# A two-layer decoder trunk: the overflow block of its expert stage moved to the sixth pair, scatter blocks spread among weight chunks

## The chip, the cores and the metric

The kernel runs on one core of one Trainium2 chip. The metric is the time of one launch on the device, in microseconds. A core has five engines that run their own instruction queues and meet at semaphores: TensorE (PE, with its weight loads listed as PEld), VectorE (DVE), ScalarE (ACT), GpSimd (POOL) and SyncE (SP), which here issues nearly all loads. Working memory is SBUF, matmul sums land in PSUM, weights come from HBM by DMA.

## The reference, cut to what matters

256 tokens of width 2048 pass two layers. Layer 0 mixes by retention heads beside a causal convolution, layer 1 by sparse attention. Behind each mixer come a LayerNorm and a mixture of 16 experts, of which each token uses two, and a second LayerNorm:

```
for layer in range(2):
    m = mixer(h)                                   # even: retention + convolution; odd: sparse attention
    h = layer_norm(ALPHA * h + m)
    f = sum over e of gate[:, e] * ((silu(h @ gu_a[e]) * (h @ gu_b[e])) @ down[e])
    h = layer_norm(ALPHA * h + f)
```

All is fp32. The expert weights are 16 x (2048 x 1024 + 512 x 2048) x 4 bytes = 201 MB per layer.

## The kernel before, in words

All large tiles live in 22 pages of 1 MB. Weights come in chunks of one page; `pump` (L146) issues the next load on SP while fewer than `ringmax` chunks are held and a page is free, and `done_chunk` (L167) gives a page back. So SP's queue holds the loads in the order of use, each waiting for its page and for one of eight DMA semaphores.

The dense projections of the mixers split each fp32 weight into two reduced-precision parts (`split`, L222: a copy on ACT, a subtraction on DVE or POOL) and multiply three ways (`mm`, L242). `dense` (L272) runs the units in order.

An expert stage (`moe`, L821) first routes the tokens. Each expert takes up to 64 tokens; `back` (L836) copies the normalised input h into token rows of two pages. The 16 experts go in eight pairs (loop at L1016). For pair i:

- `gather` (L866) picks the tokens of both experts by matmuls with a one-hot matrix, h being the stationary side, in four blocks c; `gates` (L880) makes the matrices for the way back.
- `gu` (L897) is the first product of one expert: eight chunks, two columns of PE's array used side by side, into one PSUM bank; then SiLU on ACT and a product on DVE.
- `turn` (L914) transposes the result, ACT copies it to gT, and `down` (L934) multiplies by four chunks of the second weight. `weigh` (L924) scales by the gate into Y, hi part on ACT and lo part on DVE.
- `scatter` (L967) adds pair i's results to the rows of all tokens: eight blocks of four matmuls (`placed`, L950) and one DVE addition each (`spread`, L957). It runs in pair i + 1 behind the first `gu`, four blocks before the transpose and four after it.

Gathers of the next pair stand behind the first `down` and around the second transpose. Behind the last pair's second `gu` come `turn`, `overflow` and `last_down`. `overflow` (L1060) holds the general way for experts with more than 64 tokens, inside a conditional (L1070) on a count that is read into registers in pair 1; with these inputs it is branched past. Engines go through it one by one: PE, ACT and DVE branch and then set their semaphore to what the block would have left, and SP does so for each of the eight DMA semaphores, waiting first until the loads counted on it have landed. `overflow` takes three pages. `last_down` (L975) finishes the last expert column block by column block: `begin` puts the old sums of blocks 2 and 3 into PSUM by a matmul with the identity, four down products follow, each with `weigh`, and `finish` places the block and takes its LayerNorm statistics. In layer 0 two units of the next dense stage are split early within it.

In layer 1 of the trunk `fold` (L1115) normalises, transposes and scales two of sixteen column blocks at a time, `parts` (L1121) splits them, and the first dense matmuls start behind `parts(0)`. `norms` (L700) decides which quarter of the rows is normalised when.

Of the kernel before, what the change touches and what calls it, by code (L numbers as in the profile page):

```python
# [19 lines left out]
P = 128  # L20
# [9 lines left out]
TAPS = 31  # L30

# [49 lines left out]
class Trunk:  # L81
# [618 lines left out]
    def norms(self, kp):  # L700

        for c in ((0, 1), (2,), (3,))[kp] if kp < 3 else ():
            self.norm(c)
# [117 lines left out]
    def moe(self, layer, before_last=None):  # L821
# [14 lines left out]
        def back(t, c):  # L836
# [5 lines left out]
            o = h[t][:, c * 512:(c + 1) * 512]  # L842
# [23 lines left out]
        def gather(i, c):  # L866


            ps = self.psum("psg")
            for b in range(4):  # L870
                q, r = divmod(c * 4 + b, 2)
                for t in range(2):
                    f = h[t].rearrange("p (q j r) -> p q r j", q=8, r=2)[:, q, r, :]
                    nc.tensor.matmul(ps[:, b * P:(b + 1) * P], f, self.PT[i][:, t, 0:P], start=t == 0, stop=t == 1)
# [22 lines left out]
        def gu(i, j):  # L897
            ps = self.bank("pgu")
            for c in range(8):
                if i == 0 and j == 0 and c in (2, 4):  # L900
                    gather(0, c // 2 + 1)
# [55 lines left out]
        def spread(i, t, c):  # L957
# [3 lines left out]
            if i == 0:  # L961
                V.scalar_tensor_tensor(z, h[t][:, c * 512:(c + 1) * 512], ALPHA, ps, op0=ALU.mult, op1=ALU.add)
# [4 lines left out]
        def scatter(i, t):  # L967
            if i == 0 and t == 0:
                self.acc = [self.page(f"z{t}") for t in range(2)]
            for c in range(4):  # L970
                spread(i, t, c)
            if t == 1:
                self.drop(2)

        def last_down(gT, early):  # L975

            begun = {}

            def begin(b, alloc):

                for t in range(2):
                    ps = begun[b, t] = alloc("psb")
                    nc.tensor.matmul(ps, self.ident, self.acc[t][:, b * 512:(b + 1) * 512], start=True, stop=False, skip_group_check=True)  # L983
# [12 lines left out]
            begin(2, self.bank)  # L996
            ws = [self.take() for b in range(4)]
            for b in range(4):
# [8 lines left out]
                for half in range(2):  # L1007
                    weigh(7, 1, half, po, b * 256)
                for u in early if b == 2 else ():
                    self.split(u, nc.gpsimd)  # L1010
                    self.early.append(u)
                if b:
                    finish(b - 1)
                if b == 1:
                    begin(3, self.psum)
            finish(3)  # L1016
            self.drop(2)

# [4 lines left out]
        for i in range(8):  # L1023
            if i == 7:
                self.ringmax = 8
            if 0 < i < 7:
# [3 lines left out]
            sl = gu(i, 0)  # L1030
            if i:
                scatter(i - 1, 0)
# [369 lines left out]
```

## Time and profile before

| what | value |
|---|---|
| time, median of 3 runs | 1712.36 us (1707.39 to 1713.14) |
| the profiled execution | 1710.37 us, of it 1708.6 us span |
| mean granted TensorE clock | 0.983 of full |
| PE busy | 1639.9 us, 96% of the span |
| DVE, ACT, POOL busy | 743.3, 499.5, 345.4 us |
| moved by DMA | 528 MB, 309 GB/s over the span |
| first expert stage | from about 385 to 872 us |
| second expert stage | from about 1205 to 1692 us |
| split of a dense unit | ACT 1045 ns, POOL 2535 ns, DVE 1547 ns, means of the page |

Times within the span are counted from its start. In the rows below a line names its place in the code (L907 is line 907), its engine, the tile written and the tiles read, the partitions and elements, and how many instructions of the kind stand together. A time in brackets is idle time of the engine before the instruction, with the engine or transfer that ended it. TensorE matmuls overlap one another, so the distance of two starts says more than a duration.

### The profile page before, as it was taken

The numbers are of one execution on the slowest core, as the hardware profiler recorded it, in microseconds if no ns is written. First come the engines' busy times: TensorE is split into PE (matmuls) and PEld (weight loads), VectorE is DVE, ScalarE is ACT, GpSimd is POOL, SyncE is SP. The second block draws the span as 40 slices with busy tenths as digits, with TensorE's granted clock in tenths as the row PEclk, the third lists the DMA queues.
The fourth block names the chain that finished last, engine by engine and source line by source line (L and its number), as shares of the span: only waits on it lengthen the run. The fifth ranks groups of instructions, "written<-read, shape, count | busy, mean of one in ns | idle before, by whom it ended". The sixth has DMA issues, their size and how long they took to land. (4 is left out here: it accounts for less than half of the span.)

```text
span 1708.6 us, 21350 instructions
## 1 busy us (share of the span) xinstructions
PE 1639.9 (96%) x8551; PEld 1039.2 (61%) x8551; DVE 743.3 (44%) x1348; ACT 499.5 (29%) x780; POOL 345.4 (20%) x218
## 2 busy tenths in 40 slices
PE   9999999999999999999789999999999999999984
PEld 7888887786454445444268788788644445454432
DVE  5699987533123222221264675664412212232225
ACT  5434345433111111111054535553311111111101
POOL 1446664540000000000024554444000000000010
PEclk9999999999999999999989999999999999999996
DMA  9655545858999999999954554357899999999992
GB/s 341 216 196 173 172 148 192 304 197 353 376 411 421 421 421 420 422 420 420 407 186 139 171 176 145 124 200 267 319 358 416 422 420 421 421 421 420 421 413 76
DMA packets 122860, 528.29 MB, mean 309 GB/s; under 512 B 10506, under 2 KB 10898, under 8 KB 74498
## 3 DMA queue, kind: packets, MB, share of 16 engines
q1 hardware_dynamic: 122130, 525.32, 79.1%
q8 instruction: 71, 1.16, 0.3%
q0 software_dynamic: 480, 1.46, 0.2%
q14 instruction: 35, 0.29, 0.0%
q10 hardware_dynamic: 144, 0.07, 0.0%
HBM read 524.71 MB, written 2.10 MB: 308 GB/s over the span
## 5 line engine op out<-in xcount | busy, mean ns | idle before, releaser
L907 PE MATMUL pgu<-w,X 128*64 128x512 f32 x2048 | 449.8, 594 | 7.3 <-DMA w<-in_moe_w_gu_dram 7.3
L237 POOL TENSOR_TENSOR sp<-w,sp 128x1024 fp32r<-128x1024 f32 (+1 forms) x108 | 272.9, 2535 | 398.9 <-ACT sp L234 383.4
L907 PEld LDWEIGHTS pgu<-w,X 128*64 128x64 f32 x2048 | 144.0, 137 | 295.2 <-issue 267.3
L234 ACT ACTIVATE sp<-w 128x1024 fp32r<-128x1024 f32 (+1 forms) x228 | 230.4, 1045 | 121.4 <-PE acc L268 64.1
L237 DVE TENSOR_TENSOR sp<-w,sp 128x1024 fp32r<-128x1024 f32 (+1 forms) x120 | 185.3, 1547 | 129.4 <-ACT sp L234 129.1
L932 DVE SCALAR_TENSOR_TENSOR Yl<-pdn,gs,Yh 64x512 fp32r<-64x512 f32 (+1 forms) x136 | 97.7, 718 | 272.2 <-ACT Yh L931 271.2
L942 PE MATMUL pdn<-w,gT 128*64 128x512 f32 x960 | 212.6, 595 | 0.9 <-ACT gT L919 0.9
L931 ACT ACTIVATE Yh<-pdn,gs 64x512 fp32r<-64x512 f32 (+1 forms) x136 | 89.4, 657 | 306.9 <-PE pdn L942 213.0
L911 DVE TENSOR_TENSOR sl<-sl,pgu 128x256 f32<-128x256 f32 x32 | 13.5, 422 | 352.1 <-ACT sl L910 352.1
L266 PE MATMUL acc<-sp,xhi 128*128 128x512 f32 x384 | 152.2, 396 | 0.0
L267 PE MATMUL acc<-sp,xhi 128*128 128x512 f32 x384 | 149.7, 390 | 0.3 <-DVE sp L237 0.3
L268 PE MATMUL acc<-sp,xlo 128*128 128x512 f32 x384 | 149.8, 390 | 0.0
L792 POOL COPY pt<-pt 128x128 f32<-128x128 f32 x16 | 5.1, 317 | 707.1 <-DVE pt L791 707.1
L942 PEld LDWEIGHTS pdn<-w,gT 128*64 128x64 f32 x960 | 66.3, 137 | 123.4 <-issue 117.1
L910 ACT ACTIVATE sl<-pgu 128x256 f32<-128x256 f32 x32 | 12.3, 385 | 385.2 <-PE pgu L907 385.2
L470 DVE SCALAR_TENSOR_TENSOR pcv<-up,cw,pcv 128x255 f32<-128x255 f32 (+14 forms) x240 | 113.2, 472 | 7.3
L266 PE MATMUL acc<-sp,hhi 128*128 128x512 f32 x256 | 106.0, 414 | 1.2 <-ACT hhi L1125 1.2
L268 PE MATMUL acc<-sp,hlo 128*128 128x512 f32 x256 | 101.0, 395 | 1.2 <-DVE hlo L1126 1.2
L267 PE MATMUL acc<-sp,hhi 128*128 128x512 f32 x256 | 100.5, 393 | 0.0
L267 PEld LDWEIGHTS acc<-sp,xhi 128*128 128x128 f32 x384 | 72.2, 188 | 15.4 <-DVE sp L237 1.0
L268 PEld LDWEIGHTS acc<-sp,xlo 128*128 128x128 f32 x384 | 72.1, 188 | 15.3
L266 PEld LDWEIGHTS acc<-sp,xhi 128*128 128x128 f32 x384 | 72.2, 188 | 14.8 <-ACT sp L234 0.4
(305 smaller groups left out, 2067.8 us busy)
## 6 DMA issues: line engine op xcount, KB each, us to landing
w<-in_moe_w_gu_dram SPq DMA_DIRECT2D x256, 1024.0 KB, 16.5
w<-in_moe_w_down_dram SPq DMA_DIRECT2D x128, 1024.0 KB, 19.5
w<-in_even_w_in_dram SPq DMA_DIRECT2D x46, 1024.0 KB, 5.5
w<-in_odd_w_in_dram SPq DMA_DIRECT2D x32, 1024.0 KB, 5.2
w<-in_even_w_out_dram SPq DMA_DIRECT2D x16, 1024.0 KB, 8.7
w<-in_odd_w_out_dram SPq DMA_DIRECT2D x16, 1024.0 KB, 5.3
acc<-in_x_dram SPq DMA_DIRECT2D x8, 256.0 KB, 8.3
w<-in_even_w_in_dram SPq DMA_DIRECT2D x4, 512.0 KB, 6.7
```

The lines of the kernel that those rows point to most:

```text
L234: nc.scalar.activation(sp[:, 0], src, AF.Copy)
L237: eng.tensor_tensor(sp[:, 1], src, sp[:, 0].bitcast(F32), ALU.subtract)
L266: nc.tensor.matmul(ac, xh[:, x], wh, start=st, stop=False)
L267: nc.tensor.matmul(ac, xh[:, x], wl, start=False, stop=False)
L268: nc.tensor.matmul(ac, xl[:, x], wh, start=False, stop=en)
L470: nc.vector.scalar_tensor_tensor(y, up[:, c, 0:S - i], w, y, op0=ALU.mult, op1=ALU.add)
L907: nc.tensor.matmul(ps[h * 64:(h + 1) * 64, :], X[i][:, k, j * 64:(j + 1) * 64], wv[:, kk, :, h, :], start=k == 0, stop=k == KT - 1)
L910: nc.scalar.activation(sl, ps[:, 0:256], AF.Silu)
L911: V.tensor_tensor(sl, sl, ps[:, 256:512], ALU.mult)
L931: nc.scalar.activation(hi, po[r, :], AF.Copy, scale=g)
L932: V.scalar_tensor_tensor(lo, po[r, :], g, hi.bitcast(F32), op0=ALU.mult, op1=ALU.subtract)
L942: nc.tensor.matmul(po[b][half * 64:(half + 1) * 64, :], gT[:, c, h * 64:(h + 1) * 64], wv[:, half ^ j, 2 * b:2 * b + 2, :], start=kk == 0, ...
```

## The change

- `overflow` now stands behind the sixth pair (i = 5, `GENERAL`): that pair's second transpose and down product come first, then the block, then all gathers and the gates of the seventh pair. It uses two pages (one for weights instead of two); the two pages of h are given back at the top of the last pair. The ring is held at 14 chunks in the sixth pair and 16 after it.
- The eight blocks of a scatter are handed to the first `gu` of the next pair: one ahead of each of its chunks 2 to 7, one behind it before the transpose, one behind the transpose.
- `back` writes h in the order of the weights' rows, so a gather reads contiguous columns; the first scatter, which reads h, does so in two pieces of half the width through strided views.
- `begin` for blocks 2 and 3 runs ahead of chunks 3 and 5 of the last pair's second `gu`.
- The last `weigh` takes the upper half first; one unit instead of two is split early, and behind the four down products; ten warm-up matmuls follow `last_down`; the rows of the last LayerNorm are loaded before the last `gu`; `norms` takes one quarter per call.

```diff
@@ norms
-        for c in ((0, 1), (2,), (3,))[kp] if kp < 3 else ():
-            self.norm(c)
+        if kp < 4:
+            self.norm(kp)
@@ back
-            o = h[t][:, c * 512:(c + 1) * 512]
+            o = h[t][:, c * 512:(c + 1) * 512].rearrange("p (q r j) -> p q r j", q=2, r=2)
+            ps = ps.rearrange("p (q j r) -> p q r j", q=2, r=2)
@@ gather
-                q, r = divmod(c * 4 + b, 2)
-                for t in range(2):
-                    f = h[t].rearrange("p (q j r) -> p q r j", q=8, r=2)[:, q, r, :]
-                    nc.tensor.matmul(ps[:, b * P:(b + 1) * P], f, self.PT[i][:, t, 0:P], start=t == 0, stop=t == 1)
+                k = c * 4 + b
+                for t in range(2):
+                    nc.tensor.matmul(ps[:, b * P:(b + 1) * P], h[t][:, k * P:(k + 1) * P], self.PT[i][:, t, 0:P], start=t == 0, stop=t == 1)
@@ gu
-        def gu(i, j):
+        def gu(i, j, also=None):
             ps = self.bank("pgu")
             for c in range(8):
+                if also and c in also:
+                    also[c]()
...
@@ spread
             if i == 0:
-                V.scalar_tensor_tensor(z, h[t][:, c * 512:(c + 1) * 512], ALPHA, ps, op0=ALU.mult, op1=ALU.add)
+                for q in range(2):
+                    s = slice(q * 256, (q + 1) * 256)
+                    v = lambda x: x[:, s].rearrange("p (j r) -> p j r", r=2)
+                    V.scalar_tensor_tensor(v(z), h[t][:, c * 512:(c + 1) * 512][:, s].rearrange("p (r j) -> p j r", r=2), ALPHA, v(ps),
+                                           op0=ALU.mult, op1=ALU.add)
@@ scatter
-        def scatter(i, t):
-            if i == 0 and t == 0:
-                self.acc = [self.page(f"z{t}") for t in range(2)]
-            for c in range(4):
-                spread(i, t, c)
-            if t == 1:
-                self.drop(2)
+        def scatter(i):
+            def first():
+                if i == 0:
+                    self.acc = [self.page(f"z{t}") for t in range(2)]
+                spread(i, 0, 0)
+            def last():
+                spread(i, 1, 3)
+                self.drop(2)
+            return [first] + [lambda c=n // 2, t=n % 2: spread(i, t, c) for n in range(1, 7)] + [last]
@@ last_down
-            begin(2, self.bank)
...
-                for half in range(2):
+                for half in (1, 0):
                     weigh(7, 1, half, po, b * 256)
-                for u in early if b == 2 else ():
-                    self.split(u, nc.gpsimd)
-                    self.early.append(u)
                 if b:
                     finish(b - 1)
-                if b == 1:
-                    begin(3, self.psum)
+            for u in early:
+                self.split(u, nc.gpsimd)
+                self.early.append(u)
             finish(3)
             self.drop(2)
+            self.warm(10)
@@ the loop over pairs
+            if i == GENERAL:
+                self.ringmax = 14
             if i == 7:
                 self.ringmax = 8
+                self.drop(2)
...
-            sl = gu(i, 0)
             if i:
-                scatter(i - 1, 0)
+                sc = scatter(i - 1)
+                sl = gu(i, 0, {c: sc[c - 2] for c in range(2, 8)})
+                sc[6]()
                 gT = turn(sl)
-                scatter(i - 1, 1)
+                sc[7]()
...
             down(i, 0, gT)
-            if i < 7:
+            if i < 7 and i != GENERAL:
                 gather(i + 1, 0)
                 gather(i + 1, 1)
-            sl = gu(i, 1)
-            if i < 7:
+            if i == 7 and before_last:
+                before_last()
+            sl = gu(i, 1, {3: lambda: begin(2, self.bank), 5: lambda: begin(3, self.psum)} if i == 7 else None)
+            if i == GENERAL:
+                down(i, 1, turn(sl))
+                self.overflow(layer, rv, h, wide)
+                self.ringmax = 16
+                self.pump()
+                for c in range(4):
+                    gather(i + 1, c)
+                gates(i + 1)
+            elif i < 7:
...
-        gT = turn(sl)
-        self.overflow(layer, rv, h, wide)
-        if before_last:
-            before_last()
-        last_down(gT, self.units([Group(512, None, None)])[:2] if layer == 0 else ())
+        last_down(turn(sl), self.units([Group(512, None, None)])[:1] if layer == 0 else ())
@@ overflow
-        ow = [self.page(f"ow{i}") for i in range(2)]
+        ow = self.page("ow")
...
-        self.drop(5)
+        self.drop(2)
```

## Rows read from the trace of the kernel before

**Rows 1.** by stretch: busy us (instructions) of five engines, granted clock, DMA share, GB/s
```profile
465.00:826.00 361.00, 361.00 (x1968) 173.17 (x1966) 92.68 (x165) 56.90 (x99) 1.95 (x6) 1.00 1.01 420
...
850.00:856.00 6.00, 5.68 (x14) 2.41 (x16) 0.00 (x0) 0.00 (x0) 0.00 (x0) 0.50 1.05 386
...
858.00:866.00 8.00, 7.93 (x56) 4.72 (x52) 5.26 (x10) 3.05 (x6) 0.00 (x0) 1.00 0.54 177
...
879.50:883.40 3.90, 3.89 (x9) 3.08 (x10) 2.50 (x5) 2.93 (x5) 0.00 (x0) 0.50 0.00 0
```

**Rows 2.** PE in order of time, a pair of experts: start, us, what
```profile
632.07 13.90 PE L907 MATMUL pgu<-w,X 128*64 128x512 f32 x64
...
645.90 0.38 PE L954 MATMUL psa<-Yh,gtt 128*128 128x256 f32 x1
...
647.91 0.38 PE L917 MATMUL pst<-cst,sl 128*128 128x128 f32 x2
...
650.44 7.09 PE L942 MATMUL pdn<-w,gT 128*64 128x512 f32 x32
...
657.46 4.04 PE L874 MATMUL psg<-pt,acc 128*128 128x128 f32 x32
...
661.43 13.96 PE L907 MATMUL pgu<-w,X 128*64 128x512 f32 x64
...
679.40 0.60 PE L887 MATMUL psp<-cst,pt 128*128 128x128 f32 x4
...
687.64 0.60 PE L907 MATMUL pgu<-w,X 128*64 128x512 f32 x2
```

**Rows 3.** what PE waited for in each expert stage: us, times, longest
```profile
PE pgu L907 <- DMA w<-in_moe_w_gu_dram: 3.3, 6, 0.6
...
PE pgu L907 <- DMA w<-in_moe_w_gu_dram: 4.0, 8, 0.7
```

**Rows 4.** PE in order of time, end of the second expert stage
```profile
1660.75 1.94 PE L907 MATMUL pgu<-w,X 128*64 128x512 f32 x8 [0.65 <-DMA w<-in_moe_w_gu_dram]
...
1663.63 0.44 PE L917 MATMUL pst<-cst,sl 128*128 128x128 f32 x2 [0.94 <-DVEq L1070]
...
1679.43 1.88 PE L983 MATMUL psb<-z,cst 128*128 128x512 f32 x4
...
1681.24 1.95 PE L1005 MATMUL pdn<-w,gT 128*64 128x256 f32 x16
...
1683.12 0.39 PE L954 MATMUL psa<-Yh,gtt 128*128 128x256 f32 x1
...
1684.27 1.95 PE L1005 MATMUL pdn<-w,gT 128*64 128x256 f32 x16
```

**Rows 5.** ACT in order of time, the same place
```profile
1664.16 0.38 ACT L919 ACTIVATE gT<-pst 128x256 f32<-128x256 f32 x1 [1.04 <-PE pst L917]
```

**Rows 6.** PE, first product of the first pair, interrupted by gathers
```profile
407.60 3.65 PE L907 MATMUL pgu<-w,X 128*64 128x512 f32 x16
...
425.95 0.66 PE L887 MATMUL psp<-cst,pt 128*128 128x128 f32 x4
```

**Rows 7.** DVE in order of time, behind a down product
```profile
633.64 1.53 DVE L932 SCALAR_TENSOR_TENSOR Yl<-pdn,gs,Yh 64x512 fp32r<-64x512 f32 x2 [0.75 <-ACT Yh L931]
...
635.92 0.76 DVE L932 SCALAR_TENSOR_TENSOR Yl<-pdn,gs,Yh 64x512 fp32r<-64x512 f32 x1 [0.75 <-ACT Yh L931]
```

**Rows 8.** single lines: count, then ns least/median/most
```profile
L874 PEld LDWEIGHTS psg<-pt,acc x512: 193/197/197, 403.6 to 790.3; 128*128 128x128 f32 x171
...
L887 PE MATMUL psp<-cst,pt x64: 272/273/328, 425.9 to 1609.8; 128*128 128x128 f32 x64
...
L890 PEld LDWEIGHTS pgs<-gate,pt x128: 190/192/192, 426.3 to 1610.6; 128*128 128x128 f32 x128
...
L844 ACT ACTIVATE acc<-psh x6: 582/605/630, 400.7 to 403.1; 128x512 f32<-128x512 f32 x6
```

**Rows 9.** the branch past the conditional block, PE's sequencer: count, ns
```profile
L1070 PEldq COMPARE_BRANCH  x2: 6194/6326/6457, 843.7 to 1663.6; - x2
```

More of the change, by code (lines that the diff above doesn't have):

```diff
@@ L30 @@
 TAPS = 31
+GENERAL = 5
 C_ID, C_IOTA, C_TRI, C_SEL, C_KW, C_LOW, C_CAUS, C_N = 0, 128, 192, 320, 336, 352, 368, 496
@@ L965, in spread, with begin @@
             return z
-        def scatter(i, t):
-            if i == 0 and t == 0:
-                self.acc = [self.page(f"z{t}") for t in range(2)]
-            for c in range(4):
-                spread(i, t, c)
-            if t == 1:
-                self.drop(2)
-        def last_down(gT, early):
-            begun = {}
-            def begin(b, alloc):
-                for t in range(2):
-                    ps = begun[b, t] = alloc("psb")
-                    nc.tensor.matmul(ps, self.ident, self.acc[t][:, b * 512:(b + 1) * 512], start=True, stop=False, skip_group_check=True)
+        def scatter(i):
[5 more added lines that the diff above has]
+                spread(i, 1, 3)
+                self.drop(2)
+            return [first] + [lambda c=n // 2, t=n % 2: spread(i, t, c) for n in range(1, 7)] + [last]
+        begun = {}
+        def begin(b, alloc):
+            for t in range(2):
+                ps = begun[b, t] = alloc("psb")
+                nc.tensor.matmul(ps, self.ident, self.acc[t][:, b * 512:(b + 1) * 512], start=True, stop=False, skip_group_check=True)
+        def last_down(gT, early):
             def finish(b):
@@ L1023, in moe @@
         for i in range(8):
+            if i == GENERAL:
+                self.ringmax = 14
             if i == 7:
                 self.ringmax = 8
+                self.drop(2)
             if 0 < i < 7:
                 self.onehot(i + 1)
-            sl = gu(i, 0)
             if i:
-                scatter(i - 1, 0)
+                sc = scatter(i - 1)
+                sl = gu(i, 0, {c: sc[c - 2] for c in range(2, 8)})
+                sc[6]()
                 gT = turn(sl)
-                scatter(i - 1, 1)
+                sc[7]()
             else:
+                sl = gu(i, 0)
                 self.onehot(1)
@@ L1079, in overflow @@
                     for ab in range(2):
-                        w = ow[ab].rearrange("p (c n) -> p c n", c=KT)
+                        w = ow.rearrange("p (c r n) -> p c r n", c=8, r=2)
                         c0 = ab * FF + f * P
-                        nc.sync.dma_start(w, wg[ds(e, 1), :, c0:c0 + P].rearrange("o (c p) n -> p (o c) n", p=P))
+                        for r in range(2):
+                            nc.sync.dma_start(w[:, :, r, :], wg[ds(e, 1), :, c0:c0 + P].rearrange("o (c p r) n -> r p (o c) n", p=P, r=2)[r])
                         for k in range(KT):
-                            nc.tensor.matmul(ps[:, ab * S:(ab + 1) * S], w[:, k, :], at(k), start=k == 0, stop=k == KT - 1)
+                            nc.tensor.matmul(ps[:, ab * S:(ab + 1) * S], w[:, k // 2, k % 2, :], at(k), start=k == 0, stop=k == KT - 1)
                     nc.scalar.activation(gT[:, 4 + f, :], ps[:, 0:S], AF.Silu)
@@ L1088, in overflow @@
                 for c in range(4):
-                    w = ow[c % 2].rearrange("p (c n) -> p c n", c=4)
+                    w = ow.rearrange("p (c n) -> p c n", c=4)
                     nc.sync.dma_start(w, wd[ds(e, 1), :, c * 512:(c + 1) * 512].rearrange("o (c p) n -> p (o c) n", p=P))
```

## The prediction

> **What bounds the kernel now.** I read the page's slices first; both expert stages stand out there by their rate of loading. Whether that is the limit isn't said by a rate, so the next view is the table by stretch: for 361 us of the first expert stage PE is busy 361.00 us at the full clock while 420 GB/s flow [rows 1]. The PE rows of one pair of experts settle which of the two sets the pace. A pair takes 687.64 - 632.07 = 55.57 us [rows 2]. Its 24 loads of 1.049 MB need 24 x 1.049 / 0.420 = 59.9 us. So PE eats 4.3 us per pair out of the ring of prefetched chunks, and PE, not DMA, is the bound until the ring is empty. It is empty only at the very end: in the eighth pair PE waits for loads at eight chunks of the second layer (six in the first), at the 2.5 us spacing of the loads instead of 13.83 / 8 = 1.73 [rows 2, 3]. That is 6 x 0.77 = 4.6 us of stall in the first layer; in the second, by the idle time seen (4.0 against 3.3), 5.6. Then come the conditional block and the tail.
>
> So the reader is to see a PE-bound stage with some 5 us of slack per layer at its end, and a tail of 24.3 us behind the last down product (1684.27 to 1708.6 [rows 4]) that nothing here shortens.
>
> **The change, per layer.** All sums are against the profiled execution's own 1710.37 us (span 1708.6 and 1.8 around it); the median of the three runs shown is 2.0 above it.
>
> *Spread blocks among chunks (seven pairs).* Today eight blocks stand between the first product and its down product: 650.44 - 645.90 = 4.54 us, four blocks taking 2.01, so 0.50 each [rows 2]. They cover the latency of SiLU, product, transpose and copy. Uncovered, as at the end of the second layer, these cost: a group of eight started at 1660.75 would hand over at 1662.56 or so (1.81 later), the transpose came at 1663.63, so 1.07; the copy of gT ended 0.91 after it (1664.16 + 0.38), so with its hand-over 0.96 [rows 4, 5]. Two blocks of 0.5 fit inside these 2.03 us, so this stretch shrinks by 2.5. Six blocks move into the product: 6 x 0.50 = 3.0, plus a seam for each. The price of a seam stands in the one place where PE already leaves the product midway: 64 matmuls with two gather groups took 425.95 - 407.60 = 18.35 us, against 13.83 + 3.97 = 17.80 for the same work in two pieces [rows 2, 6]; 0.55 for two interruptions, of which a part is the slower first group. I take 0.22 each, 1.3 for six. Net 3.0 + 1.3 - 2.5 = +1.8 us per pair, **+12.6** for seven. Bounds: no seam 0.5 per pair (+3.5); the seam at 0.28 and a wait of 1.2 for Y in each pair 3.4 (+24). That wait: the first block is issued 2 x 1.71 = 3.4 us into the product; its half of Y is there at 634.4 (third DVE piece starts there), 2.3 us in, the whole of Y 4.6 us in (635.92 + 0.76 [rows 7]). I take the half, since the last pair's blocks already read one part of Y while ACT writes the next.
>
> The Trainium skill ("TensorE: Matmul & The Clock Gate", section Part 2) has TensorE pull the next weight load ahead of running matmuls when it goes to the background buffer. By that the seams cost nothing, the term is 3.5 instead of 12.6, and the sum below turns to -8 us; the 0.55 us of the interrupted product speak against it.
>
> *h in weight-row order.* A gather's weights are read contiguously instead of every second element. The nearest contiguous matmuls of the same size are four transposes that span 0.60 us, 0.27 of it the last one's own: one each 0.110. 32 gather matmuls span 4.04; with the same 0.27 for the last, one each 0.122 [rows 2, 8]: 64 x 0.012 = 0.8 us per pair. By the weight loads alone it is 197 against 192 ns [rows 8], 0.3 per pair. I take 0.6, nearer to the pace, eight times: **-5** (bounds 0 and -6.4). The price is paid in the copies of h out of PSUM, which now read every second element: six of 0.605 us on ACT per layer [rows 8]. No row shows a strided PSUM read; between 0 and a doubling (+3.6) I take 0, the contiguous row being the nearest. The first scatter's 16 half-size DVE operations in place of 8 lie beside 14 us of products; twice 0.68 us a block would still hide.
>
> The Trainium skill ("Advanced Engine Details and Errata", section Memory Cachelines) says that two hits on a 16-byte SBUF line keep full speed, and that PSUM wants two neighbouring fp32 values. By it a stride of two costs the gather nothing, so there is nothing to win, while the new PSUM read is the slow kind: the sum below is then +20 instead of +10. The 5 ns of the loads lean towards the page, the 0.122 against 0.110 away from it.
>
> *Overflow block behind pair 6.* PE's branch past the block took 6.2 and 6.5 us [rows 9]. Now it stands in the middle of a PE-bound stage: 6.3. There the gathers of the next pair no longer cover SiLU and gT: 2.03 - 0.22 for the transpose, 1.8. After the same pause in the tail the granted clock was 0.50 of full (1.2 GHz) from 850 to 856 us [rows 1]; PE's 5.7 us of work in it lose 2.8. Together **+10.9** (8.1 if the clock stays up, 13 if it stays down twice as long). SP also runs into the block: in the first layer it waits there until its eight loads have landed, and between 858 and 866 us the loads move 177 GB/s, (420 - 177) x 8 / 420 = 4.6 us lost [rows 1]. What is queued behind SP there are only later loads. PE has fourteen chunks allotted when it enters; its pause, gathers and gates take some 18 us, twelve chunks another 27, the SP drain (8 x 2.5 = 20) and the first new landing (5) are over 20 us before PE wants the fifteenth. So this stall costs nothing while PE is late.
>
> *Old sums into PSUM amid the last product.* Eight matmuls at the full clock, 1.81 for four [rows 4], plus two seams: **+3.8** in the product (bound 0, if PE still waits for loads there). They leave the tail.
>
> *Slack.* PE comes later to the last product, so the loads are there: **-4.6** and **-5.6**. With the terms above PE reaches the last chunk 12.6 - 5 + 10.9 + 3.8 = 22.3 us later than without stalls, 16.7 after today's time in layer 2; the load, delayed by 4.6, comes 12 us before that.
>
> *Tail from the transpose to the last down product.* Today 1684.27 - 1663.63 = 20.6 us in the second layer; I take the first as equal. Without branch and sums, at the full clock: 0.96, three down products of 1.88, two pairs of placed blocks of 1.15, and 0.3 of waiting for the first of them: 9.2 [rows 4]. **-11.4**.
>
> *Start of the odd layer.* One normalisation leaves the front (under 1 us), ten warm-up matmuls fill part of PE's gap before the transposes, and 3.9 us of dense matmuls ran at 0.50 of the clock [rows 1]; up to -4. Against it: only one unit is split early, so the second unit's split (1.05 us of ACT and 2.5 of POOL by the means of the page, queued behind the second block's parts) comes some 6 us after the first matmul, which at the full clock needs it after 3: +3. I take **-1** (from -4 to +3). The warm-up of the second layer and the earlier row loads lie beside DVE's last work.
>
> **Sum.** Layer 2: 12.6 - 5 + 10.9 + 3.8 - 5.6 - 11.4 = +5.3. Layer 1: the same with 4.6, less 1: +5.3. Together +10.6: 1721.0 on the profiled execution, 1723.0 on the median; I forecast 1721. In short, the block moves from one PE-critical place to another, and what is left is seams against gathers.
>
> **Rivals.**
> A, faster: *the seams vanish*, since weights for the next kind of matmul load behind the running one. Place: the six switches in each of 14 first products; price 18.2 us less: 1703. It decides once a seam costs under 0.1 us. For it: weight loads do overlap in steady runs. Against: the interrupted product. 20%.
> B, *no visible change*: gathers gain their 6, the clock stays up behind the block, seams at 0.18: 2 + 5.6 + 3.4 = 11 off the sum, 1712 on the median. 25%.
> C, slower than forecast: *the first spread block waits for all of Y*, PE in order behind it: 14 x 1.2 = 17 us, 1738; or the gathers gain nothing, 1731. For it: Y is one tile per half. Against: reads of parts in the last pair. 13% together.
> D, *the block starves PE*: were PE not late, SP's drain would show as a stall of up to 4.6 us per layer; it needs A to be true, and is inside it.
> My forecast has the remaining 42%.
>
> A measurement of this kernel can tell about 0.3%, 5.1 us. Faster than that: A, 0.20. Within: B, 0.25. Slower: the forecast and C, 0.55. The range runs from A at 1704 to C's 1737. The likeliest case's own range is 1716 to 1728.
>
> **What would show it.** PE still without waits up to the last product, and no wait for loads in it either. The pair period rising from 55.6 to about 56.8 us; first products of 18 us with six groups of four psa matmuls inside; gather groups of 32 under 3.97 us. PE's branch of about 6.3 us behind the sixth pair, a stretch at 0.50 of the clock after it, and a dip in GB/s some 25 us later. 9 to 10 us from the last transpose to the last down product. I am wrong if PE waits for loads in the eighth pair (then the stage is DMA-bound and the tail's gain stays), if the pair period doesn't rise, or if psa in the product waits for DVE.

## The result and the profile after

The changed kernel takes **1733.74 us** (median of four runs, 1731.84 to 1734.31) against 1710.57 before: ratio 1.0134, 95% interval 1.0113 to 1.0156. It is slower, as forecast, and inside the range; but the forecast was 1721, a loss of 10.6 us on the profiled execution where 23.4 came (span 1732.0 against 1708.6).

First the table by stretch of the changed kernel, columns as in [rows 1]: the second to seventh pair of the first layer with the first 7 us of the eighth, then the gathers behind the overflow block, and two stretches at the start of the odd stage.

```profile
466.00:826.00 360.00, 351.87 (x1856) 162.16 (x1852) 91.48 (x163) 54.25 (x93) 1.93 (x6) 0.99 1.00 413
...
748.80:755.50 6.70, 4.54 (x21) 4.57 (x22) 1.21 (x2) 1.28 (x2) 0.00 (x0) 0.50 1.02 415
...
890.30:895.20 4.90, 4.87 (x12) 3.77 (x13) 2.54 (x5) 3.94 (x6) 1.15 (x1) 0.50 0.00 0
902.40:905.50 3.10, 3.10 (x8) 2.48 (x8) 1.75 (x3) 1.35 (x4) 0.00 (x0) 0.50 0.21 52
```

PE is still the engine that sets the stage: busy 351.87 of 360 us, and most of the other 8 lie at the block. In 360 us it does 1856 matmuls, where 361 us held 1968 [rows 1]. In the waits of PE in the first expert stage and the turn behind it (us in all, times, longest) no wait for a load is left, nor is there one in the second stage; there were 3.3 and 4.0 us [rows 3]:

```profile
PE psg L875 <- DVEq L1090: 4.6, 1, 4.6
PE pst L920 <- DVE sl L914: 3.8, 9, 0.9
...
PE pdn L945 <- ACT gT L922: 1.0, 2, 0.5
```

So the loss is PE's own work and its order. One pair shows it. PE of the changed kernel in order of time, to be held against [rows 2]:

```profile
580.74 3.60 PE L910 MATMUL pgu<-w,X 128*64 128x512 f32 x16
584.27 0.38 PE L957 MATMUL psa<-Yh,gtt 128*128 128x256 f32 x1
...
592.54 1.94 PE L910 MATMUL pgu<-w,X 128*64 128x512 f32 x8
594.41 0.39 PE L957 MATMUL psa<-Yh,gtt 128*128 128x256 f32 x1
594.63 0.28 PE L957 MATMUL psa<-Yl,gtt 128*128 128x256 f32 x1
594.75 0.28 PE L957 MATMUL psa<-Yh,gtt 128*128 128x256 f32 x1
594.87 0.28 PE L957 MATMUL psa<-Yl,gtt 128*128 128x256 f32 x1
595.08 1.94 PE L910 MATMUL pgu<-w,X 128*64 128x512 f32 x8
...
600.49 0.44 PE L920 MATMUL pst<-cst,sl 128*128 128x128 f32 x2 [0.28 <-DVE sl L914]
...
601.46 7.09 PE L945 MATMUL pdn<-w,gT 128*64 128x512 f32 x32
608.48 3.84 PE L875 MATMUL psg<-pt,acc 128*128 128x128 f32 x32
612.25 13.95 PE L910 MATMUL pgu<-w,X 128*64 128x512 f32 x64
...
638.26 2.31 PE L910 MATMUL pgu<-w,X 128*64 128x512 f32 x10
```

The pair takes 638.26 - 580.74 = 57.52 us; it took 55.57. From the first product's start to the down product: 601.46 - 580.74 = 20.72 against 650.44 - 632.07 = 18.37 [rows 2], **2.35 us more**. The gathers behind the down product: 612.25 - 608.48 = 3.77 against 3.97; over the pair's three groups 0.39 less. 2.35 - 0.39 is the 1.95 by which the period grew.

A single place inside the product: a chunk of eight matmuls takes 594.41 - 592.54 = 1.87 us before it hands over to the block, where eight take 13.83 / 8 = 1.73 when the product runs through; the block takes 595.08 - 594.41 = 0.67, where blocks in a row take 0.50. So one interruption costs 0.14 + 0.17 = **0.31 us**, not 0.22. The starts tell where the second part sits: the block's first matmul is followed after 0.22 us and the others after 0.12, and the product resumes 0.21 after the last. The weight loads (PEld) of the same place:

```profile
594.41 0.19 PEld L957 LDWEIGHTS psa<-Yh,gtt 128*128 128x128 f32 x1 [0.81 <-issue]
594.52 0.19 PEld L957 LDWEIGHTS psa<-Yl,gtt 128*128 128x128 f32 x1
...
595.08 0.20 PEld L910 LDWEIGHTS pgu<-w,X 128*64 128x64 f32 x4
```

Inside the block a load starts 0.11 us ahead of its matmul (594.52 and 594.63). The block's first load starts with its matmul (594.41), and so does the product's first one behind the block (595.08): at a change of kind no load ran ahead.

Where the 23.4 us come from, in the two layers (forecast in brackets): spread blocks 7 x 2.35 = +16.45 each (12.6); gathers -3.1 each (-5); the sixth pair's excess over the fifth +8.4 and +9.1 (10.9); old sums +4.1 each (3.8); loads' waits -4.6 and -5.6 (the same); tail from the transpose to the last down product 9.3 us in both instead of 21.1 and 20.6, so -11.8 and -11.3 (-11.4); the start of the odd stage +3.8 (-1; measured below). That is 9.5 + 9.7 + 3.8 = 23.0. The rest is two short falls of the clock that come and go between runs, +1.15 ahead of the first expert stage and -0.95 in the odd stage.

### The profile page after: what moved, and what is told of

It reads as the page before. It is cut to its first block, busy times and chain, and to the rows that moved or that the text cites. A ratio compares the mean times of both kernels' runs of the same rounds, so it can differ in the third digit from the quotient of the medians.

```text
span 1732.0 us, 21420 instructions
## 1 busy us (share of the span) xinstructions
PE 1668.2 (96%) x8571; PEld 1037.4 (60%) x8571; DVE 756.9 (44%) x1364; ACT 499.1 (29%) x780; POOL 347.2 (20%) x218
## 5 line engine op out<-in xcount | busy, mean ns | idle before, releaser
L910 PE MATMUL pgu<-w,X 128*64 128x512 f32 x2048 | 466.0, 597 | 0.0
L910 PEld LDWEIGHTS pgu<-w,X 128*64 128x64 f32 x2048 | 137.4, 136 | 247.2 <-issue 230.6
L239 DVE TENSOR_TENSOR sp<-w,sp 128x1024 fp32r<-128x1024 f32 (+1 forms) x120 | 189.9, 1586 | 130.5 <-ACT sp L236 130.1
L971 DVE TENSOR_TENSOR z<-psa,z 128x512 f32<-128x512 f32 x104 | 71.7, 690 | 112.3 <-PE psa L957 112.0
L957 PEld LDWEIGHTS psa<-Yh,gtt 128*128 128x128 f32 x240 | 45.0, 188 | 81.9 <-issue 80.3
L269 PEld LDWEIGHTS acc<-sp,xhi 128*128 128x128 f32 x384 | 72.3, 188 | 15.4 <-DVE sp L239 1.0
```

Of the source, the lines that this page charges most:

```text
L239: eng.tensor_tensor(sp[:, 1], src, sp[:, 0].bitcast(F32), ALU.subtract)
L269: nc.tensor.matmul(ac, xh[:, x], wl, start=False, stop=False)
L910: nc.tensor.matmul(ps[h * 64:(h + 1) * 64, :], X[i][:, k, j * 64:(j + 1) * 64], wv[:, kk, :, h, :], start=k == 0, stop=k == KT - 1)
L957: nc.tensor.matmul(ps[:, o * 256:(o + 1) * 256], GT[i][0][:, o, t * P:(t + 1) * P], Y[i][n][:, o, c * 256:(c + 1) * 256], start=n == 0 and ...
L971: V.tensor_tensor(z, ps, z, ALU.add)
```

## The experiments

Theory T: the expert stage is PE's own, so each piece of PE time in the pairs counts; the interruptions are the largest piece that the forecast got too small, and the start of the odd stage is the second. R1: the block behind the sixth pair, with the drained load queue in it, holds the loss. R2: the start of the odd stage holds it. Times are medians; ratios are to the kernel before, in the same runs, with 95% intervals.

**a_behind**: the spread blocks back behind the product, in the old order.

```diff
-            return [first] + [lambda c=n // 2, t=n % 2: ...] + [last]
+            return [first] + [lambda c=n % 4, t=n // 4: ...] + [last]
...
-                sl = gu(i, 0, {c: sc[c - 2] for c in range(2, 8)})
-                sc[6]()
+                sl = gu(i, 0)
+                for f in sc[:4]: f()
                 gT = turn(sl)
-                sc[7]()
+                for f in sc[4:]: f()
```

> The changed kernel with one part undone: the eight spread blocks of a pair stand again in two fours behind the first product, before and after the transposes, instead of six of them between its chunks. Theory T (the spread blocks cost more than forecast): in the changed kernel the stretch from the first matmul of a first product to its down product is 20.72 us against 18.37 before, 2.35 us in each of 14 pairs, 33 us in all. T expects that stretch back at 18.4 us, and 1701 us if the loads keep up; the loads' waits that the kernel before had (4.6 and 5.6 us in its two layers) may come back, so 1701 to 1711. Rival R1 (the block behind the sixth pair, with the drain of the load queue in it, is what costs the most): the spread gives back no more than the 10 us by which the forecast was exceeded there, 1724 or more. Rival R2 (the start of the odd stage holds it): the same, 1724 or more.

Measured: 1702.45 us, ratio 0.9957 (0.9943 to 0.9971): 31.3 us less than the changed kernel, and faster than the kernel before. PE of this kernel in one pair:

```profile
576.76 13.90 PE L910 MATMUL pgu<-w,X 128*64 128x512 f32 x64
...
595.16 5.37 PE L945 MATMUL pdn<-w,gT 128*64 128x512 f32 x24
```

18.40 us again, and the period is 55.19. PE waits for no load in it. T holds; R1 and R2 fall as the main cause.

**a_twos**: the same six blocks, three places.

```diff
-                sl = gu(i, 0, {c: sc[c - 2] for c in range(2, 8)})
+                sl = gu(i, 0, {c: (lambda c=c: (sc[c - 3](), sc[c - 2]())) for c in (3, 5, 7)})
```

> The changed kernel with its six interleaved spread blocks in twos, ahead of chunks 3, 5 and 7 of the first product, so that there are three places where the product is interrupted in a pair and not six; all the blocks are still there. Theory T: a place costs 0.32 us whatever stands in it (chunk and block took 2.535 us in the changed kernel against 1.71 and 0.50 us by themselves), so 3 x 0.32 x 14 = 13 us less, 1720 us. Rival: the cost belongs to the block itself (its four matmuls run slower between chunks, 0.67 against 0.50 us), and stays with six blocks: 1733 us.

Measured: 1721.07 us, ratio 1.0067 (1.0048 to 1.0086). The pair takes 56.51 us, 1.01 less for three places fewer: 0.34 each. PE of this kernel:

```profile
584.20 0.39 PE L957 MATMUL psa<-Yh,gtt 128*128 128x256 f32 x1
...
585.35 3.65 PE L910 MATMUL pgu<-w,X 128*64 128x512 f32 x16
588.93 0.39 PE L957 MATMUL psa<-Yh,gtt 128*128 128x256 f32 x1
```

Two blocks together take 585.35 - 584.20 = 1.15 us, where two single ones take 1.34; two chunks together take 588.93 - 585.35 = 3.58, where two single ones take 3.74. The price is the place's and not the block's. (The 0.31 above is a little low, since the 13.83 and 2.01 it is held against each contain a change too.)

**b_scatter**: the kernel before with the interleaved blocks alone (the same edit as undone in a_behind, the other way round).

> The kernel before with one part of the change alone: six of a pair's eight spread blocks between the chunks of the first product. Theory T: seven pairs of a layer take 2.35 us more each, 16.45 us, and the loads' waits of the eighth pair (4.6 and 5.6 us) go, because PE now comes later than they do: +11.9 and +10.9, 1733 us. Rival (the forecast's own size, 1.8 us a pair): 12.6 less the same waits, 1725 us. Rival A of the prediction (no cost of a seam): 1710 us or less.

Measured: 1729.33 us, ratio 1.0119 (1.0095 to 1.0143). The period goes from 55.57 to 57.91 us, 2.34 more, and the loads' waits go. The 18 us are between the two expectations. From the first product to the last down product the first layer grew by 11.2 us in the profile, near T's 11.9, but the second by 7.0 instead of 10.9. The block still stands in the tail here, and PE's branch past it took 6.38 us in the first layer and 3.37 in the second (PE's sequencer, then the stretches of the two branches):

```profile
L1078 PEldq COMPARE_BRANCH  x2: 3374/4876/6377, 855.8 to 1685.5; - x2
```

```profile
855.80:862.20 6.40, 0.44 (x2) 0.20 (x2) 0.00 (x0) 0.38 (x1) 0.00 (x0) 0.86 0.99 364
1685.50:1688.90 3.40, 0.40 (x2) 0.17 (x2) 0.00 (x0) 0.38 (x1) 2.18 (x1) 1.00 0.02 5
```

PE was so late there that the loads had ended: 5 GB/s beside this branch, 364 beside the other. That one short branch is most of the 4 us by which T's sum was too high; by period and waits T holds. Why it was short is not shown.

**b_worder**: the kernel before with h in weight-row order alone; the first scatter reads h in halves, as in the change.

```diff
-            o = h[t][:, c * 512:(c + 1) * 512]
+            o = h[t][:, c * 512:(c + 1) * 512].rearrange("p (q r j) -> p q r j", q=2, r=2)
+            ps = ps.rearrange("p (q j r) -> p q r j", q=2, r=2)
...
-                    f = h[t].rearrange("p (q j r) -> p q r j", q=8, r=2)[:, q, r, :]
+                    nc.tensor.matmul(..., h[t][:, k * P:(k + 1) * P], self.PT[i][:, t, 0:P], ...)
```

> The kernel before with one part of the change alone: h in the order of the weights' rows, so that a gather reads its weights contiguously, the copies out of PSUM reorder, and the first scatter writes through strided halves. Theory T: the pair period falls by 0.38 us (gather groups of 32, 16 and 8 matmuls 0.20, 0.10 and 0.09 us shorter), 2.7 us in seven pairs, and PE waits that much longer for the loads in the eighth pair, since the loads set the time of the last chunk: 1710 us, within 2 us. Rival (the stage is bound by PE to its end): 1705 us. Rival (the copies out of PSUM with a stride of two cost twice): 1714 us.

Measured: 1707.08 us beside 1711.38, ratio 0.9981 (0.9968 to 0.9994). The period falls to 55.19, by 0.38 as expected, and PE comes to the eighth pair 2.9 us earlier. PE's waits for loads in this kernel, first and second layer:

```profile
PE pgu L907 <- DMA w<-in_moe_w_gu_dram: 5.0, 10, 0.6
...
PE pgu L907 <- DMA w<-in_moe_w_gu_dram: 6.0, 11, 0.7
```

They were 3.3 and 4.0 [rows 3]: 1.7 and 2.0 us of the gain are handed over to the loads, not all of it. The result is 0.9 us below T's band and 2 us above the PE-bound rival: neither holds as it stood.

**a_noblock**: the changed kernel without the overflow block, its branch and general path; the pages that it takes stay free.

```diff
-                self.overflow(layer, rv, h, wide)
+                wide("ohT", S), wide("ohT", S)
```

> The changed kernel without the block for overflowing experts (its branch, and so its general path, is left out; its two buffers are still taken, so that the rotation of buffers is the same, and the sixth pair keeps its order without overlap). Theory T: the pause of the branch (4.8 us from the end of the down product to the gathers beyond what other pairs show) and the half clock in the gathers behind it (2.0 and 2.7 us) go, the uncovered 1.7 us of the sixth pair stays: 7 us in each layer, 1720 us. Rival R1 (the block with the drained load queue starves later pairs too): more than the stretch itself, 1712 us or less. Rival: the pause only takes the place of waits for loads that would come anyway: 1730 us or more.

Measured: 1717.22 us, ratio 1.0049 (1.0032 to 1.0066). The sixth pair takes 59.03 instead of 65.92 us, and 59.04 instead of 66.65 in the second layer: 6.9 and 7.6 us, as T had it. What is left of its excess, 1.5, is the uncovered SiLU and gT. The other 2 us of the 16.5 are, by the two profiles, falls of the clock outside the experts.

**a_turned**: in the sixth pair the transposes ahead of the block, the down product behind it.

```diff
-                down(i, 1, turn(sl))
+                gT = turn(sl)
                 self.overflow(layer, rv, h, wide)
+                down(i, 1, gT)
```

> The changed kernel with the sixth pair's transposes and copy of gT ahead of the block, and its last down product behind it. In the changed kernel PE's gathers come 4.6 us after the down product, when DVE has done the last of four weighing steps. Theory T (the branch itself takes PE 6.3 us, and hides in the changed kernel under the running down product; only the weighing shows there): the down product starts 6.3 us after the transposes instead of 0.8, the gathers follow it at once instead of 4.6 us later: 0.5 to 1.5 us more in each layer, 1735 to 1737 us. Rival (the branch is short, and the pause is the weighing alone, which now stands beside PE's work): 3 to 4 us less in each layer, 1726 to 1728 us.

Measured: 1735.19 us, ratio 1.0142 (1.0112 to 1.0171). PE of the changed kernel at the block, then of this one:

```profile
738.26 0.44 PE L920 MATMUL pst<-cst,sl 128*128 128x128 f32 x2 [0.94 <-DVE sl L914]
739.23 7.09 PE L945 MATMUL pdn<-w,gT 128*64 128x512 f32 x32 [0.53 <-ACT gT L922]
750.96 9.58 PE L875 MATMUL psg<-pt,acc 128*128 128x128 f32 x64 [4.64 <-DVEq L1090]
```

```profile
738.50 0.44 PE L920 MATMUL pst<-cst,sl 128*128 128x128 f32 x2 [0.94 <-DVEq L1091]
744.84 9.05 PE L945 MATMUL pdn<-w,gT 128*64 128x512 f32 x32 [5.89 <-DMA w<-in_moe_w_gu_dram]
753.82 7.41 PE L875 MATMUL psg<-pt,acc 128*128 128x128 f32 x64
```

744.84 - 738.50 = 6.34 us from the transposes to the down product, and the sixth pair is 0.43 and 0.44 us longer in the two layers. (The profile puts the 5.89 down to a load, the one that came last.) The branch of PE's sequencer, in the changed kernel and in this one:

```profile
L1090 PEldq COMPARE_BRANCH  x2: 5947/6013/6079, 741.9 to 1573.2; - x2
```

```profile
L1091 PEldq COMPARE_BRANCH  x2: 5969/5993/6017, 738.5 to 1569.8; - x2
```

T holds. In the changed kernel the branch starts at 741.9, while PE still works on the down product, and is over some 6 us later; what shows is the time until DVE has done the last weighing step. DVE there, in the changed kernel:

```profile
747.72 1.53 DVE L935 SCALAR_TENSOR_TENSOR Yl<-pdn,gs,Yh 64x512 fp32r<-64x512 f32 x2 [0.75 <-ACT Yh L934]
750.00 0.76 DVE L935 SCALAR_TENSOR_TENSOR Yl<-pdn,gs,Yh 64x512 fp32r<-64x512 f32 x1 [0.75 <-ACTq L1090]
```

It ends at 750.76, PE's gathers start at 750.96.

**b_block**: the kernel before with the block behind the sixth pair, on one page fewer, with the gathers, ring sizes and pages given back as in the change; old sums in the tail.

```diff
+            if i == 5:
+                down(i, 1, turn(sl))
+                self.overflow(layer, rv, h, wide)
...
         gT = turn(sl)
-        self.overflow(layer, rv, h, wide)
```

> The kernel before with one part of the change alone: the block for overflowing experts behind the sixth pair instead of ahead of the last down product, with one load page fewer; the old sums still enter PSUM in the tail. Theory T: about 9 us more at the sixth pair, the tail from the transpose to the last down product 13 instead of 21 us, and the loads' waits of the eighth pair (4.6 and 5.6 us) gone: -4 in each layer, 1702 us. Rival R1 (the drain of the load queue behind the block brings waits for loads that are dearer than the forecast had it): 1712 us or more.

Measured: 1700.20 us, ratio 0.9945 (0.9924 to 0.9966). The sixth pair grows by 7.7 and 7.5 us, the tail falls to 11.9 us in both layers, and of the waits one of 0.6 is left in each:

```profile
PE pgu L907 <- DMA w<-in_moe_w_gu_dram: 0.6, 1, 0.6
```

R1 falls here for good: taken alone, the moved block is a gain of 5.6 us a layer.

**a_oddold**: the start of the odd stage as before.

```diff
-        if kp < 4:
-            self.norm(kp)
+        for c in ((0, 1), (2,), (3,))[kp] if kp < 3 else ():
+            self.norm(c)
...
-            for u in early:                     # behind the last down product, one unit
+                for u in early if b == 2 else ():   # amid it, two units
...
-            self.warm(10)
...
-        last_down(turn(sl), ...[:1] if layer == 0 else ())
+        last_down(turn(sl), ...[:2] if layer == 0 else ())
```

> The changed kernel with the turn from the first expert stage to the odd stage put back: two units split early on GpSimd amid the last down product instead of one behind it, the norms of columns in the old order, and no ten warming matmuls. Theory T: the milestones of the dense product lost 3.8 us between the end of the expert stage and its third unit, so 1730 us; not below 1727. Rival R2 (the odd start holds most of what the forecast lacked, about 10 us): 1724 us. Rival R3 (the old order is worse here, since the shorter tail leaves less time for two splits): 1735 us or more.

Measured: 1728.48 us, ratio 1.0117 (1.0091 to 1.0142). I take the stretch from the start of the last down product to the 114th matmul of the dense product, in its tenth unit: 47.31 us before, 51.12 in the changed kernel, 47.04 here. The 3.8 us are lost in this turn, and the old edits bring them back. Three single edits and one pair:

**a_early2** (two units behind the down product: `[:1]` to `[:2]`), **a_nowarm** (without `self.warm(10)`), **a_norms** (the old order of the norms alone), **a_amid** (two units amid the down product, new norms, warming kept).

> The changed kernel with two units split early behind the last down product instead of one. In the changed kernel the odd stage's start loses 3.8 us from the last down product to its fifth unit: PE stands for 2.2 us where DVE, sharing the time with GpSimd's late split of the second unit, is late with a norm, and runs 3.1 us at half clock behind that. Theory T (the one early unit is the cause): those 3.8 us go, 1730 us. Rival (the half clock at the first dense matmuls, there already, is the cause): no change in this loss, 1733 to 1734 us.

> The changed kernel without the ten warming matmuls behind the expert stage. They take 4.0 us (at half clock) of a gap of 9.5 us in which PE waits for the norms. Theory T: they neither delay the first transposes nor spare the half clock at the first dense matmuls, so nothing changes within 1 us: 1733 to 1734 us, and the start of the odd stage loses the same 3.8 us. Rival (they keep the clock from falling further): 2 us or more longer. Rival (they hold up the transposes): 1 to 3 us shorter.

> The changed kernel with the old order of the norms: two groups of columns before the first transposes, none before the fourth. Theory T: the norm that DVE was late with (2.6 us beside GpSimd) is then done before GpSimd's split starts; the 2.2 us gap goes and with it the half clock behind it, while the first transposes come up to 1 us later: 3 to 4 us less, 1730 us. Rival (only the split itself holds PE up): no change, 1733 to 1734 us.

> The changed kernel with its two early units split amid the last down product, as before; norms in the new order and the warming matmuls stay. From the last down product to the dense product's fifth unit the changed kernel loses 3.8 us, with two units behind the down product 5.1, with the old norms alone 2.3, with everything old -0.3. Theory T (the place of the early splits on GpSimd is what counts: amid the down product it is done with both before the columns' statistics come, and has no split left for the time in which DVE has norms): 0.5 to 1.5 lost, 1730 to 1731 us. Rival (the order of the norms is what counts): 2 to 4 lost, 1732 to 1734 us.

Measured: 1735.62, 1734.15, 1731.13 and 1731.22 us, two runs each. In that stretch they take, in one profile each, 52.45, 51.38, 49.60 and 47.95 us: +5.1, +4.1, +2.3 and +0.6 against the kernel before, where the changed kernel has +3.8. Of the four, a_early2 was a miss: with two splits ahead of them the columns' statistics come later on GpSimd, and the first transposes 2.3 us later. a_norms got 2.6 of the 3 to 4 us that its T expected. The ten warming matmuls do nothing for the time, as T had it: they run at half clock themselves, and in these two traces the dense product starts at half clock with or without them.

The others make a square (its corner with both old, a_oddold, also lacks the warming matmuls): new norms with the late split +3.8, old norms with the late split +2.3, new norms with two splits amid the down product +0.6, both old -0.3. So the place of the splits is worth 2.6 to 3.2 us and the order of the norms 0.9 to 1.5. The norms first: GpSimd, then DVE, of the changed kernel.

```profile
894.05 5.71 POOL L239 TENSOR_TENSOR sp<-w,sp 128x1024 fp32r<-128x1024 f32 x2 [8.28 <-ACT sp L236]
```

```profile
890.92 0.54 DVE L687 TENSOR_SCALAR z<-z,mv,rs 128x512 f32<-128x512 f32 x1
...
894.95 2.56 DVE L239 TENSOR_TENSOR sp<-w,sp 128x1024 fp32r<-128x1024 f32 x1 [1.20 <-ACT sp L236]
897.44 2.61 DVE L687 TENSOR_SCALAR z<-z,mv,rs 128x512 f32<-128x512 f32 x1
...
902.60 1.23 DVE L239 TENSOR_TENSOR sp<-w,sp 128x1024 fp32r<-128x1024 f32 x1 [0.25 <-ACT sp L236]
```

While GpSimd splits, DVE's own split takes 2.56 us instead of 1.23, and the last norm 2.61 where the one before took 0.54. PE stands for about 2 us until what DVE and ACT do behind that norm is done, and the clock is at half from 902.4 to 905.5 (the table at the top). With the old order this norm is done before GpSimd starts, and 0.9 us is left of the gap, where PE waits for the split itself; in a_amid, with the new order, it is there, behind the third unit's split.

The place of the splits acts by the split itself. With one unit split early, the lower part of the second unit's weights is the first of the two splits in the 894.05 row, and PE gets to it about when it is done. That the half clock at the first dense matmuls (890.3 to 895.2, the table at the top) hides this wait, a_noblock shows. Its code is the changed kernel's here, but its first dense matmuls run at full clock, and PE then waits for GpSimd:

```profile
882.60:886.90 4.30, 4.21 (x17) 2.78 (x17) 2.30 (x4) 3.33 (x6) 0.49 (x1) 1.00 0.01 2
```

```profile
886.38 0.50 PE L268 MATMUL acc<-sp,hhi 128*128 128x512 f32 x1
888.82 0.50 PE L269 MATMUL acc<-sp,hhi 128*128 128x512 f32 x1 [1.93 <-POOL sp L239]
```

The same matmul in the changed kernel:

```profile
896.49 0.50 PE L269 MATMUL acc<-sp,hhi 128*128 128x512 f32 x1
```

Counted from the start of the last down product (867.57 and 875.22) it comes after 21.25 and 21.27 us: the full clock gains nothing. In a_amid, with two splits amid the down product, it comes after 18.2.

Nor does the clock follow the place. It was at half there before [rows 1], and is so in b_block, both with two splits amid the down product; it is full in a_oddold, with the same place. b_block, then a_oddold, by stretch:

```profile
874.00:877.60 3.60, 2.99 (x7) 2.37 (x8) 1.86 (x4) 2.63 (x6) 0.00 (x0) 0.50 1.10 349
```

```profile
888.10:893.00 4.90, 4.90 (x22) 3.79 (x23) 3.49 (x6) 3.62 (x5) 0.24 (x1) 1.00 0.00 0
```

What sets the clock at this place these runs don't show.

**best1**: a_behind and a_oddold in one; what is left of the change is the moved block, the order of h, the old sums in the last product and two small edits (the upper half first in the last `weigh`, the earlier row loads). **best2**: b_block and b_worder in one, so without the old sums there and without the small edits.

> The changed kernel with two parts undone together: the spread blocks stand behind the first product in fours, and the turn to the odd stage is as before (two units split early amid the last down product, old order of norms, no warming matmuls). What is left of the change is h in weight-row order, the block behind the sixth pair and the old sums amid the last first product. Theory T (both causes are separate and add up): 1702.4 from the first alone less 4.3 from the odd start, 1698 us. Rival (the odd start lost because the spread made GpSimd and ACT late; with the blocks behind the product it costs nothing, so putting it back gives nothing): 1702 us.

> The kernel before with two parts of the change only: h in weight-row order, and the block behind the sixth pair. The spread blocks stand behind the first product, the old sums enter PSUM in the tail, the odd stage starts as before. Against the version with the old sums amid the last first product (1698.1 us) this prices that one part: it puts 4.1 us into the product (18.98 us with the sums against 14.9) and takes the tail from the transpose to the last down product from 11.9 to 9.3 us, since in the tail the first four of these matmuls cover the copy of gT. Theory T: a net loss of 1.5 us in each layer, so 1695 us without it. Rival (loads: with these sums gone PE reaches the last chunks sooner than they land, and waits): 1698 to 1700 us.

Measured: best1 **1698.11 us**, ratio 0.9931 (0.9910 to 0.9953); best2 1699.29 us, ratio 0.9925 (0.9911 to 0.9938). Both beat both kernels; which of the two is faster these runs don't tell, nor whether they are faster than b_block alone (1700.20): nearly all of the gain is the moved block. The two causes of best1 add up, as T had it. In best2 the rival was right: PE, earlier at the last product without the sums, waits for loads there, 1.7 and 1.9 us:

```profile
PE pgu L907 <- DMA w<-in_moe_w_gu_dram: 1.7, 3, 0.6
...
PE pgu L907 <- DMA w<-in_moe_w_gu_dram: 1.9, 4, 0.6
```

Where the old sums stand is then worth nothing that can be measured, the small edits included: 4.1 us in the product against 2.6 in the tail and the waits.

## Why the prediction was right in sign and wrong in size

**Spread blocks: the step that failed.** "I take 0.22 each." The mechanism and the other terms of this step hold: the blocks are read in PE's order, the first one doesn't wait for Y, and the uncovered stretch behind the product took 1.98 us (2.03 forecast). The term that failed is the size of the seam: 0.31 by the changed kernel's rows, 0.34 by a_twos, instead of 0.22. Six of them in 14 pairs make the term 2.35 us a pair instead of 1.8, 7.7 of the 12.8 us that the forecast lacks. The row that it came from [rows 6] gave 0.55 for two interruptions, 0.28 each; I argued a part of it away as the slow first group, with nothing that showed it. Rival A's place is settled too. The Trainium skill ("TensorE: Matmul & The Clock Gate", section Part 2) lets the next weights load ahead of running matmuls when they go to the background buffer, and the prediction took an interruption to be free by that. Here 42 places fewer gave 12.7 us back, 0.30 each, and at a change between these two kinds of matmul the first weight load starts with its matmul and not ahead of it; which buffer it goes to no row shows.

**h in weight-row order**: right in sign, -3.1 instead of -5 a layer. The pace of the four transposes was the wrong neighbour; the loads' own 197 to 192 ns [rows 8] were the nearer row (186 least and 192 median in the gathers after). The Trainium skill ("Advanced Engine Details and Errata", section Memory Cachelines) lets two hits on a 16-byte line of SBUF absorb the access latency, and wants every two consecutive elements in PSUM contiguous. By that, as the prediction read it, a stride of two fp32 values is free in the gathers' weights and slow in the copies (its +20 counts the gathers alone; copies at twice the time would add up to 3.6 us a layer). The runs show neither: the gathers gained 0.20 of 3.97 us, and the copies that now read PSUM with a stride cost the same 605 ns as in [rows 8]:

```profile
L847 ACT ACTIVATE acc<-psh 128x512 f32<-128x512 f32 x6 | 3.0, 605 | 0.0
```

**Overflow block**: 10.9 forecast, 8.4 and 9.1 measured. The branch isn't paid in full; it starts under the running down product, and DVE's weighing sets the 4.6 us that show (a_turned). The half clock behind it came as forecast, 6.7 us long. Rival D's stall did not come, not even in a_behind, where PE has no seams to be late with. The block came out 4.3 us cheaper in the two layers and the gathers gained 3.8 less: that these two misses nearly cancel is luck.

**Old sums, slack, tail**: 4.1 for 3.8, no wait left, 9.3 for 9.2. These held. The summary sentence behind the sum, that "the block moves from one PE-critical place to another", did not: with the loads' waits it was the part most worth having, 11 us in b_block (h in weight-row order alone gave 4).

**Start of the odd stage**: -1 forecast (bounds -4 to +3), +3.8 measured, 4.8 us of the miss. The late second split was seen, and its +3 is what the place of the splits measures (2.6 to 3.2). What failed is what it was set off against: the first dense matmul comes 15.1 us after the last down product, where it came after 14.7, the warming matmuls buy no time, and at full clock PE only waits longer for the split (a_noblock). One thing was not seen: DVE takes more than twice as long beside GpSimd, which makes a norm late that looked covered (0.9 to 1.5). Both edits are priced by the square above; what sets the clock there is open.

## What to carry to other kernels

In a stage where one engine is busy all the time, work put between its instructions isn't hidden by anything: price the change of kind itself, from a place where the kernel already does it, and multiply by the number of places before anything else. Where work must be interleaved, few places with much in each are cheaper than many. A price seen once for two places is to be taken whole, unless a row shows what else is in it. And before a stretch at half clock is counted as a loss, look at what the engine would wait for at full clock.

## What the runs showed of the hardware

- A change from the first product's matmuls (128 x 64 weights, 512 columns) to a block's (128 x 128 weights, 256 columns) and back costs PE 0.31 to 0.34 us at the full clock: 0.14 ahead of the block, 0.10 behind its first matmul, and 0.09 at the way back, by the starts above. The first weight load behind each change starts with its matmul; inside the block a load starts 0.11 us ahead. Which of the differences between the two kinds counts isn't shown.
- A copy of 128 x 512 fp32 out of PSUM with a stride of two elements takes ACT 605 ns, as a contiguous one does; 128 x 128 weights with that stride cost PE 0.20 us in 32 gather matmuls.
- PE's branch past the block took 5.9 to 6.5 us in both kernels and in a_turned, and 3.37 once, where the loads beside it had ended (second layer of b_scatter). It is covered as far as PE still has a product running when it comes to it.
- DVE beside a busy GpSimd: 2.56 us instead of 1.23 for a subtraction of 128 x 1024, 2.61 instead of 0.54 for a norm of 128 x 512.
